# New orders of steps in four stages of a two-block transformer kernel

## The chip, the cores and the metric

The kernel runs as one launch on one core of a Trainium2 chip. The metric is device time in microseconds (us); lower is better.

## The reference

512 tokens of 1024 channels in float32 go through two blocks. The first is adaLN, one input projection, stick-breaking attention beside a Mamba-2 recurrence (SSD), and an output projection. The second is RWKV-7 time mixing, a convolutional FFN, sparse attention that chooses keys by an index score, and another FFN. Cut to what the four stages compute:

```python
# attention and SSD
log_beta = jax.nn.log_sigmoid(z)
log_one_minus = jnp.where(mask, jax.nn.log_sigmoid(-z), 0.0)
tail = lax.cumsum(log_one_minus, axis=3, reverse=True) - log_one_minus
weights = jnp.exp(jnp.where(mask, log_beta + tail, -jnp.inf))
y = ssd_scan(xs, dt, a, b_in, c_in, d_skip)
# time mixing: the front (shift, mix, projections), then the recurrence
xx = token_shift(x) - x
xm = x[None] + xx[None] * mix[:, None, None, :]
r, k, v = jnp.einsum('nbsd,nde->nbse', xm[:3], w_rkv)
state = (state * w_t[:, :, None, :] + sa[..., None] * b_t[:, :, None, :]
         + v_t[..., None] * k_t[:, :, None, :])
# sparse attention
score = jnp.einsum('bths,bth->bts', jax.nn.relu(s_idx), wi_b)
_, sel = lax.top_k(score, topk)
o_lat = jnp.einsum('bhtk,btkc->bthc', p, kv_sel)
```

## The kernel before

The program goes through its stages one after the other: input projection (to 112 us of the profiled execution), attention and SSD (112 to 475), output projection with its residual (475 to 587), the front of time mixing (587 to 697), the recurrence with time mixing's output projection (697 to 1140), the first FFN (1140 to 1570), sparse attention (1570 to 1819) and the last FFN (1819 to the end).

Each matrix product is made of three: a weight tile `raw` comes by a DMA that SP issues, ACT copies it to a rounded half `whi` (L213; in the front L1107), DVE or POOL subtracts to get the rest `wlo` (L216; L1109), and PE multiplies `whi` by the input's half `xh`, `whi` by `xl` and `wlo` by `xh` (L229, L229, L230). `raw` has three buffers, `whi` and `wlo` two each (four where the stage has room).

In four stages the work is split into generators, and a string of letters with counts says whose next step is written when: `run_order` (L119) takes a letter, and asks that generator for as many steps as the count says; what is left over at the string's end is written then. Within these stages the order of PE, DVE, ACT and POOL is the written one, so each engine works through its own list from the top and stops at an instruction that waits. The generators are:

- attention (`ATT_ORDER`): d dense products of the projection, z scores of a unit (L619 to L630), t its transposes (L641 to L647), v its product with the values (L660), g gates, s SSD.
- the front (`FRONT_ORDER`): t first half of a mixed input tile (DVE L1034 makes `xf`, ACT L1043 rounds it to `xh`), u its lower half `xl` (L1064, on POOL or DVE), v tiles of the values' input, w weights, d dense products, e their copies and the hidden layers (ACT L1167 to L1176, DVE L1161 to L1180), r the rest of the stage before: the norm's factors of the second 256 tokens (`factors2`, DVE L788 to L794, from sums that ACT makes in L779), their transposes (PE L802, then DVE L810 or ACT L807), and the four residual rows (ACT L815, then POOL L816).
- the recurrence (`ORDER`): l the small products of decay and rate (PE L1376 and L1377, ACT L1381, POOL L1383), p preparation of a unit of 64-token chunks (PE L1401 and L1411, DVE L1404 to L1455, ACT L1428, POOL L1451), g its pairwise products (PE L1474), i and h, v its triangular inverses, f and c the fold and the chain over chunks, t the tail, x input tiles for the second 256 tokens, d dense products of keys, values and the output. The first inverse of a unit is 14 pairs of small POOL instructions, L1515 and L1517, each dependent on the one before. `x` shares POOL with it: DVE makes `xf` (L1232, L1233; two buffers), ACT rounds it (L1220), POOL subtracts (L1221), and only then is the buffer free again. The result of a product of 256 columns and eight input tiles (48 matmuls L229 and L230) is copied out of its bank by ACT (L1259).
- sparse attention (`DSA_ORDER`): the steps of projection, index scores, choice, softmax, transposes and values, beside dense products.

A letter has no price of its own: a `d` in the recurrence is three matmuls, in attention also three but of twice the columns.

## Time and profile before

| | |
|---|---|
| median of 3 runs | 2213.78 us |
| lowest and highest run | 2212.26 and 2217.73 us |
| profiled execution, its own time | 2211.11 us |
| its span, first to last instruction | 2209.3 us |
| mean granted TensorE clock | 0.937 of full |
| PE busy | 1955.3 us, 89% of the span |
| DVE, ACT, POOL busy | 1462.7, 940.3, 902.8 us |

The busy shares are means over stages with different limits; the clock is the share of full speed that the throttle granted to PE.

### The profile page before, as it was taken

Reading aid. Unit: us, or ns where it says so; the run is one execution under the profiler, and the core shown is the slowest. Engines: PE = TensorE matmul, PEld = TensorE weight load, DVE = VectorE, ACT = ScalarE, POOL = GpSimd, SP = SyncE. Lnnn points to the kernel's source line nnn. Section 1 sums busy time; section 2 is a strip of 40 time slices with the busy share of each in tenths; the row PEclk is TensorE's granted clock in tenths of the full one; section 3 lists DMA queues with packets and bytes.
Section 4 is the critical chain, followed back from the end, with each engine's and each line's share of the span. In section 5 each row is a group of like instructions: output and inputs, shape, how many; then the busy total and the mean of one; then the engine's idle time right before and its main releaser. Section 6 shows DMA issues by size and latency. Waiting matters only on the chain.

```text
span 2209.3 us, 35729 instructions
## 1 busy us (share of the span) xinstructions
PE 1955.3 (89%) x14064; PEld 1631.0 (74%) x14064; DVE 1462.7 (66%) x2824; ACT 940.3 (43%) x1633; POOL 902.8 (41%) x787
## 2 busy tenths in 40 slices
...
GB/s 277 97 82 80 86 78 76 87 96 96 95 117 93 74 66 83 74 71 98 74 123 144 105 99 100 96 96 65 150 29 58 68 117 84 96 96 96 153 115 57
DMA packets 88856, 212.44 MB, mean 96 GB/s; under 512 B 23728, under 2 KB 36192, under 8 KB 88688
## 3 DMA queue, kind: packets, MB, share of 16 engines
...
q14 instruction: 57, 0.47, 0.1%
...
## 4 chain that ended last, share of the span: by engine, by line
PE 35%; DVE 14%; issue 8%; POOL 6%; ACT 3%; DMA 2%; POOLq 0%; DVEq 0%; ACTq 0%; SPq 0%
PE ps_pj L229 8%; PE ps_acc L229 7%; PE ps_pj L230 4%; PE ps_acc L230 3%; PE ps_w L229 3%; POOL wlo L216 2%; PE ps_w L230 1%; PE ps_kp L229 1%; DVE wlo L216 1%; POOL B L1517 1%; POOL b L1515 1%; ACT whi L213 1%; DVE rs_t L319 1%; DVE rs_t L320 1%; DMA raw<-in_w_up_dram 1%
## 5 line engine op out<-in xcount | busy, mean ns | idle before, releaser
L216 POOL TENSOR_TENSOR wlo<-raw,whi 128x1024 fp32r<-128x1024 f32 (+2 forms) x153 | 371.4, 2428 | 773.7 <-ACT whi L213 744.1
L213 ACT ACTIVATE whi<-raw 128x1024 fp32r<-128x1024 f32 (+2 forms) x276 | 290.0, 1052 | 491.9 <-PE ps_w L230 225.0
L216 DVE TENSOR_TENSOR wlo<-raw,whi 128x1024 fp32r<-128x1024 f32 (+1 forms) x123 | 162.1, 1318 | 268.7 <-ACT whi L213 266.9
L229 PE MATMUL ps_pj<-hh,whi 128*128 128x512 f32 x368 | 156.3, 425 | 1.7 <-ACT whi L213 1.7
L1920 DVE SCALAR_TENSOR_TENSOR fc<-ps_acc,pv,fc 128x511 f32<-128x511 f32 x88 | 65.9, 749 | 133.2 <-ACT fc L1918 131.6
L230 PE MATMUL ps_pj<-hh,wlo 128*128 128x512 f32 x368 | 145.1, 395 | 1.7 <-DVE wlo L216 1.7
L229 PE MATMUL ps_pj<-hl,whi 128*128 128x512 f32 x368 | 144.5, 393 | 0.0
L229 PE MATMUL ps_w<-wlo,ah 128*128 128x512 f32 x352 | 136.9, 389 | 0.6 <-POOL wlo L216 0.6
L229 PE MATMUL ps_w<-whi,ah 128*128 128x512 f32 x352 | 136.9, 389 | 0.0
L230 PE MATMUL ps_w<-whi,al 128*128 128x512 f32 x352 | 136.8, 389 | 0.0
L229 PE MATMUL ps_kp<-xh,whi 128*128 128x256 f32 x256 | 86.2, 337 | 12.7 <-ACT v L1259 9.0
L628 DVE TENSOR_TENSOR_SCAN cx<-om,zero 128x127 f32<-128x127 f32 (+3 forms) x64 | 74.1, 1158 | 34.2 <-ACT om L626 34.0
L229 PE MATMUL ps_pj<-x0h,whi 128*128 128x512 f32 (+1 forms) x192 | 73.9, 385 | 11.1 <-DVE x0h L305 6.1
L230 PEld LDWEIGHTS ps_pj<-hh,wlo 128*128 128x128 f32 x368 | 69.5, 189 | 18.2 <-DVE wlo L216 2.5
L229 PEld LDWEIGHTS ps_pj<-hh,whi 128*128 128x128 f32 x368 | 70.8, 192 | 14.2 <-ACT whi L213 2.6
L230 PE MATMUL ps_kp<-xh,wlo 128*128 128x256 f32 x256 | 76.3, 298 | 3.4 <-DVE wlo L216 3.3
L229 PEld LDWEIGHTS ps_pj<-hl,whi 128*128 128x128 f32 x368 | 70.1, 190 | 10.7 <-issue 0.2
L229 PEld LDWEIGHTS ps_w<-wlo,ah 128*128 128x128 f32 x352 | 66.1, 188 | 14.6 <-POOL wlo L216 1.0
L229 PE MATMUL ps_kp<-xl,whi 128*128 128x256 f32 x256 | 76.5, 299 | 0.3 <-POOL xl L1221 0.3
L229 PEld LDWEIGHTS ps_w<-whi,ah 128*128 128x128 f32 x352 | 66.1, 188 | 13.8
L230 PEld LDWEIGHTS ps_w<-whi,al 128*128 128x128 f32 x352 | 66.1, 188 | 13.6
L229 PE MATMUL ps_pj<-x1h,whi 128*128 128x512 f32 (+1 forms) x192 | 72.2, 377 | 2.4 <-DVE x1h L305 2.4
...
## 6 DMA issues: line engine op xcount, KB each, us to landing
...
```

Of the source, the lines that this page charges most:

```text
L213: self.nc.scalar.activation(hi[:, :n], raw[:, :n], AF.Copy)
L216: eng.tensor_sub(lo[:, :n], raw[:, :n], hi[:, :n])
L229: return (mm(out, wh, xh, start=first, stop=False), mm(out, wh, xl, start=False, stop=False), mm(out, wl, xh, start=False, stop=last))
L230: mm(out, wl, xh, start=False, stop=last))
L319: nc.vector.tensor_mul(t, y, y)
L320: nc.vector.scalar_tensor_tensor(t, t, -0.5, v, op0=OP.mult, op1=OP.mult)
L628: nc.vector.tensor_tensor_scan(cx[:, :n - 1][:, ::-1], om[:, 1:n][:, ::-1], K.zero.to_broadcast([128, n - 1]), 1.0, OP.mult, OP.add)
L1515: nc.gpsimd.tensor_mul(v, B[:, :s, s:s + 1].to_broadcast([64, s, n]), B[:, s:s + 1, s + 1:].to_broadcast([64, s, n]))
L1517: nc.gpsimd.tensor_add(B[:, :s, s + 1:], B[:, :s, s + 1:], v)
L1920: nc.vector.scalar_tensor_tensor(t[:, j:], pm[:, :T - j], cw(2 - j), t[:, j:], op0=OP.mult, op1=OP.add)
```

## The change

Four strings are replaced by others with the same steps: `ATT_ORDER`, `FRONT_ORDER`, `ORDER` and `DSA_ORDER`. No instruction is added, removed or moved to another engine, except that ACT loads its function tables two times less (in attention). The first line of each string in the diff:

```diff
 ATT_ORDER = (
-    "sgd2sds3ds2d2sds2dgd2sdzdz5dzsdts2dtdt2dsdtdztdz2dzds2tztzdv2s2zstzdtd3s3dtdzdzdz2dtsdt2zd2s2dt2ds2zdv2zsg"
+    "sd2s2d2sgs4d2s2d3sd2zds2z2dzdsdz2dzszdsdtdtdszsdtdtvzgsdz2dtdsztdtztd2gs2d2stzdtz2sd2svs2tztd2szdtdtztd2vd"
...
 FRONT_ORDER = (
-    "w2tutdwdtudwtdwtd3tduwudwutwd3wdt2dudwtudwtd2wd3wduwd2wdutd3er2wd2w2dur2detr2wutvrdtudwurdtuvrvdudwdtvtvw"
+    "rwt2w2tu2duwd2td3twtd2uw2dwd4twd2uwtud3wud2twuw2dudtdtdudutduwd2wet2udtr2wu2drtdtudwred2wr2drwrvd2wv3tvu2d"
...
 ORDER = (
-    "lp2d2p2dlpd4lpd7pd2ldxd3plpd4p2d7pd3pgd2pgplpdpd5gd4pl2dpd2pd2gd4gd2ildlgxi2gpdp2ixpdx2d2ihd2xilp2xiphpxih"
+    "l2p2d2ldpdxldld2pdp2dpd6p2lpd5pd7pdp2d2gd3pdpdgd4ldp2gd6pgd2plgd4xigdilidhp3dxlpdid2hdidp2xdlpxi2d2xp2dipi"
...
 DSA_ORDER = (
-    "a4qa4qdqe4d2edrqrqd3e5qde2qeqdeqede6d2e3je2j3e2de2jde2j2e2j2e2je3je2j2e3je5dj4rjd2ekejdjke3jedkejd2k2j2kek"
+    "a2qa5raqdqrq2e4qeqe2de3de2d3ede2qed2qe2de6dj2de2j2e6jejejeje2jedej3ejeje6je2jdjdejk2ekedk2jdjkjk2je3jdkj2k"
...
```

Three places show what the strings do to an engine's list.

**The start of the front, DVE.** `r` is now the string's first letter. Before, after the first half's transposes (L810):

```order
L769 SCALAR_TENSOR_TENSOR mx<-ps_w,rs_y,gateb 128x512 x2
L810 TENSOR_TENSOR xT<-ps_w,pv 128x4x128 x2
L1052 TENSOR_SCALAR xx<-xT 128x1
L1054 TENSOR_TENSOR xx<-xT 128x255
L1034 SCALAR_TENSOR_TENSOR xf<-xx,pv,xT 128x256
```

Now:

```order
L769 SCALAR_TENSOR_TENSOR mx<-ps_w,rs_y,gateb 128x512 x2
L810 TENSOR_TENSOR xT<-ps_w,pv 128x4x128 x2
L788 TENSOR_TENSOR ssqb<-ssqx 128x2
L273 TENSOR_SCALAR rmsv<-ssqb 128x2
L316 TENSOR_SCALAR rs_i<-rmsv 128x2
L317 TENSOR_SCALAR rs_y<-rs_i 128x2
...
L794 TENSOR_SCALAR dg<-cst,rs_y 128x128 x2
L1052 TENSOR_SCALAR xx<-xT 128x1
L1054 TENSOR_TENSOR xx<-xT 128x255
L1034 SCALAR_TENSOR_TENSOR xf<-xx,pv,xT 128x256
```

Fifteen small instructions (three rounds of L319, L320, L321 are left out above) moved from some forty rows later to the place ahead of the first input tile. L788 needs the last of ACT's sums L779; on ACT the last L779 and eight L807 now stand ahead of the first L1043.

**The end of the front, POOL.** Before:

```order
L1064 TENSOR_TENSOR xl<-xf,xh 128x256 x5
L816 TENSOR_TENSOR xt_4198<-xt_4198,gateb 128x1024
L1064 TENSOR_TENSOR xl<-xf,xh 128x256
L816 TENSOR_TENSOR xt_4200<-xt_4200,gateb 128x1024
L1064 TENSOR_TENSOR xl<-xf,xh 128x256 x2
L816 TENSOR_TENSOR xt_4202<-xt_4202,gateb 128x1024
L150 MEMSET pad_6181 128x1
```

Now:

```order
L816 TENSOR_TENSOR xt_4198<-xt_4198,gateb 128x1024
L816 TENSOR_TENSOR xt_4200<-xt_4200,gateb 128x1024
L1064 TENSOR_TENSOR xl<-xx,xh 128x256
L1064 TENSOR_TENSOR xl<-xf,xh 128x256 x2
L1109 TENSOR_TENSOR wlo<-raw,whi 128x1024
L1064 TENSOR_TENSOR xl<-xf,xh 128x256 x2
L816 TENSOR_TENSOR xt_4202<-xt_4202,gateb 128x1024
L1064 TENSOR_TENSOR xl<-xf,xh 128x256 x4
L150 MEMSET pad_6181 128x1
```

The residual rows moved ahead: the last four `xl` are no longer broken by one, and none stands at the end. On ACT the last L815 and the copy L1090 moved in the same way ahead of the last eight L1043.

**The recurrence, ACT around the fourth copy of a product.** Before:

```order
L1428 ACTIVATE P<-s 128x256
L1429 ACTIVATE s<-s 128x256
L1640 ACTIVATE VU<-ps_gm 64x512 x2
L1220 ACTIVATE xh<-xf 128x256
L1649 ACTIVATE BT<-ps_gm 128x512 x2
L1220 ACTIVATE xh<-xf 128x256 x3
L1658 ACTIVATE Z<-ps_gm 128x512
L1428 ACTIVATE P<-s 128x256
L1429 ACTIVATE s<-s 128x256
L1259 ACTIVATE v<-ps_kp 128x512
```

Now:

```order
L1428 ACTIVATE P<-s 128x256
L1429 ACTIVATE s<-s 128x256
L1220 ACTIVATE xh<-xf 128x256
L213 ACTIVATE l2h<-raw 128x512
L1220 ACTIVATE xh<-xf 128x256 x2
L1428 ACTIVATE P<-s 128x256
L1429 ACTIVATE s<-s 128x256
L1220 ACTIVATE xh<-xf 128x256
L1259 ACTIVATE v<-ps_kp 128x512
```

Three L1220 stand before this piece in the old order and one in the new, so the copy stands behind seven of them before and behind five now, and no longer behind L1649 and L1658. On POOL the third `xl` (L1221), which the fifth L1220 needs, stands two pairs of L1515 and L1517 ahead of the inverse's end in the new order; the fifth, which the seventh needs, stood behind that end in the old. At the start of the recurrence PE's list has also moved: the first four L1376 and L1377 now stand ahead of L1401 (before: behind L1411), and between L1401 and L1411 stand 21 dense matmuls and four small ones, where six dense ones stood. On DVE the first L1425 stands behind L1414 in both orders, and L1414 needs L1411.

At attention's end ACT's list had the last L590 behind an L608, an L645 and an L213; now the last L590 stands behind an L645 and an L213, the L608 of the product before it some five rows earlier and its own behind it. DVE's last three, L595, L596 and L647, stand as before.

## Rows read from the trace of the kernel before

**Rows 1.** Busy time by stretch; columns: busy us (instructions), granted clock, DMA share, GB/s.

```profile
core 0: us, PE busy (x) PEld busy (x) DVE busy (x) ACT busy (x) POOL busy (x), PEclk, DMA share, GB/s
112.00:475.00 363.00, 328.45 (x1955) 259.04 (x1953) 268.36 (x420) 207.36 (x358) 92.06 (x46) 0.98 0.28 87
...
587.00:697.00 110.00, 88.90 (x608) 82.44 (x608) 99.82 (x139) 57.93 (x121) 68.02 (x59) 0.89 0.31 104
697.00:1140.00 443.00, 379.73 (x5872) 336.62 (x5872) 346.04 (x766) 184.06 (x352) 250.25 (x393) 0.91 0.27 82
...
1570.00:1819.00 249.00, 199.56 (x1268) 153.89 (x1267) 174.38 (x571) 143.88 (x334) 129.06 (x115) 0.88 0.24 77
```

**Rows 2.** PE's waits from 587 to 697 us: total us, times, longest us.

```profile
PE ps_acc L229 <- DVE xl L1064: 6.5, 7, 1.5
PE ps_acc L229 <- POOL xl L1064: 3.9, 3, 2.8
```

**Rows 3.** Timeline, front's start, DVE: start us, us, what, [idle before <- releaser].

```profile
578.52 0.16 DVE L788 TENSOR_TENSOR ssqb<-ssqx 128x2 f32<-128x2 f32 x1 [0.85 <-ACT mx L779]
...
581.09 0.48 DVE L794 TENSOR_SCALAR dg<-cst,rs_y 128x128 f32<-128x128 f32 x2
...
582.81 1.41 DVE L810 TENSOR_TENSOR xT<-ps_w,pv 128x512 f32<-128x512 f32 x2
...
591.16 1.22 DVE L1109 TENSOR_TENSOR wlo<-raw,whi 128x1024 fp32r<-128x1024 f32 x1 [2.16 <-ACT whi L1107]
```

**Rows 4.** Timeline, front's start, POOL and PE: the second half's sum and the first product.

```profile
583.76 2.66 POOL L778 TENSOR_TENSOR xt<-xt,mx 128x512 f32<-128x512 f32 x2
```

```profile
587.20 0.39 PE L229 MATMUL ps_pj<-xh,whi 128*128 128x256 f32 x1 [1.94 <-ACT xh L1043]
```

**Rows 5.** Timeline, front's end: POOL, then PE, DVE and ACT.

```profile
691.23 2.38 POOL L816 TENSOR_TENSOR xt<-xt,gateb 128x1024 f32<-128x1024 f32 x1 [1.78 <-ACT xt L815]
```

```profile
688.63 0.58 PE L229 MATMUL ps_acc<-xl,whi 128*128 128x256 f32 x1 [2.80 <-POOL xl L1064]
```

```profile
690.10 0.69 DVE L1162 SCALAR_TENSOR_TENSOR hw<-lf,hw 64x512 fp32r<-64x512 f32 x1
...
691.28 2.88 DVE L1162 SCALAR_TENSOR_TENSOR ha<-lf,ha 64x512 fp32r<-64x512 f32 x1
```

```profile
694.27 0.60 ACT L1172 ACTIVATE lf<-ps_acc 128x512 f32<-128x512 f32 x1 [1.31 <-DVE ha L1162]
```

**Rows 6.** Timeline, recurrence's start: PE, then DVE.

```profile
697.73 1.87 PE L1401 MATMUL ps_gm<-cst,tmp 128*128 128x2 f32 x8 [2.19 <-ACT tmp L1396]
...
703.52 0.58 PE L230 MATMUL ps_kp<-xh,wlo 128*128 128x256 f32 x1 [3.28 <-DVE wlo L216]
```

```profile
705.02 0.34 DVE L1414 COPY rn<-ps_gm 64x8 f32<-64x8 f32 x2 [0.84 <-PE ps_gm L1411]
709.28 0.69 DVE L1425 TENSOR_TENSOR_SCAN s<-cst,s 128x256 f32<-128x256 f32 x1 [3.92 <-POOL s L1383]
```

**Rows 7.** Timeline, recurrence, the fourth copy: POOL, ACT, PE.

```profile
758.29 0.72 POOL L1221 TENSOR_TENSOR xl<-xf,xh 128x256 fp32r<-128x256 f32 x1
```

```profile
764.25 0.58 ACT L1259 ACTIVATE v<-ps_kp 128x512 f32<-128x512 f32 x1
```

```profile
752.70 1.97 PE L1655 MATMUL ps_gm<-VU,Gz 64*64 64x64 f32 x32 [0.34 <-ACT BT L1649]
...
764.88 0.58 PE L229 MATMUL ps_kp<-xh,whi 128*128 128x256 f32 x1 [8.62 <-ACT v L1259]
```

**Rows 8.** Timeline, attention's end: PE, then ACT.

```profile
472.33 2.52 PE L660 MATMUL ps_po<-at,v 128*64 128x128 f32 x16 [2.98 <-DVE at L647]
```

```profile
466.75 0.63 ACT L608 ACTIVATE sq<-xbc 128x512 f32<-128x512 f32 x1 [3.71 <-DVE xbc L596]
```

**Rows 9.** Busy time by short stretch at the recurrence's start: PE's granted clock.

```profile
697.70:708.00 10.30, 6.98 (x31) 0.50 0.47 154
```

More of the change, by code (lines that the diff above doesn't have):

```diff
@@ L701 @@
 ATT_ORDER = (
-    "sgd2sds3ds2d2sds2dgd2sdzdz5dzsdts2dtdt2dsdtdztdz2dzds2tztzdv2s2zstzdtd3s3dtdzdzdz2dtsdt2zd2s2dt2ds2zdv2zsg"
-    "zds2zdsdszsd2gtzvd3ztdsdtdzdtst2dstzdsdztsvsvt2d2tdstz2dsz2dszsz2dgtzd2ztd2stztdvgv2tdtdzdztdstzdzstdtz2dt"
-    "d2tdtzsdzdvgstvtsdz3dstzds2td2ztz2sdtdvztv2tdtzd2ts2tdtd2tztd2szgz2tsd2tds2dv2t2dzstzdzszdszszd2tdvtzszdtd"
-    "tzd2szdztdztdt2dszdzdgszvt2vz3sdgdtdvtzvdsdzsdtdz2dtdtdgds2tst2dtdzdzd2sz2szdt2dvs2vds2ztdtzd2gz3tdts2d2td"
-    "svzdtszdtvzdvtdt2dz2dtstdsd2tzd2ztd2sdzdtzv2tsdztzdtgd2vgt2d2tzds4dtds2z2dz2dgtdvzvts2zdtdtdszdzd3z2tdtdtz"
-    "tdtzsd3tzdsv2t2d2ztdz3d2zdz2dgdtvsdsdt2dtvtdtd2stz3dsdsgsdtd4td3vsd3sd66vdtd11sd7tds2tsd6vd2s2dsdvd4tsd3sd"
-    "sd2zsd5vd10sd3s"
+    "sd2s2d2sgs4d2s2d3sd2zds2z2dzdsdz2dzszdsdtdtdszsdtdtvzgsdz2dtdsztdtztd2gs2d2stzdtz2sd2svs2tztd2szdtdtztd2vd"
+    "ts2vzdtdgsvdtzs2tsdtz2d3gzdgt2sdsdzszdstdtz2dtdvtzvdstsz2dzdzts2dt2ds2gvzd2sz2dtdzs2t2sdzd2ztzvsvsz2dtd3t3"
+    "dztzdtzdz2d2sdtsdv2zdt2zsdt3dsgdtdtz2dtsdszdv2z2dz2dzt2d3szdzd2t2dtstdvztdtz2vtvs2zt2dtds2vtszdszdtdz2dsz2"
+    "sdtstdt2d2zdvstdstzd3gvsztd2zt2dv2d2zdztzdt2s3z3dzd2ztst2sdzdtztdzdszdtdzd2v2szsvdzstgtdztvz2d2t2zdtgd2t2s"
+    "dzt2zszds2zg2dgdts2tzd2zsdvtvzsd2tsdzsdsz2tdtsdtdztdsz2dzd2vd3vtstd2tdzd6t2dtz3dv2dsztz2dsdszdtdt2sgzdtzd3"
+    "stdsz2gztdsv2szdgd2s2tszd2vd2gt2dzsztd2tszd2s2dvsd2tztd2t2zdtzdt2d3sd6td6vd8td16sd3tdvtd3sd8s2dsd2sd21vd2"
+    "s3d3zd3sd3td12vd13zd15tvd3vs"
 )
```

34 lines of the change are left out of this document (17 added, 17 removed).

## The prediction

> **What bounds the kernel now.** No instruction comes or goes, so the change can only move waits. I read the busy time by stage first, then PE's waits, then the timelines of the places where the lists differ. The reader should see in the first that PE is the busy engine of three of the four stages and stands still for 363 - 328.45 = 34.6, 110 - 88.90 = 21.1, 443 - 379.73 = 63.3 and 249 - 199.56 = 49.4 us in them, 168 us in all [rows 1]; that is all an order can win besides the clock. In the front DVE is the busier one: 99.82 of 110 us. There PE's waits are many and small, 6.5 us in seven on DVE's `xl` and 3.9 in three on POOL's [rows 2]. A new string takes such waits away at some places and makes others; I therefore price the five places where the lists differ beside a wait of over 2 us, and leave the rest, with an even chance of both signs, to the range. PE's longest waits at the starts of attention and of sparse attention stand behind pieces of the lists that the strings leave as they were. The table loads that go are ACT's, which is busy 207.36 of 363 us [rows 1]: nothing.
>
> All is summed against the profiled execution's 2211.11 us; the median of the runs, 2213.78, lies 2.67 higher, which I add at the end.
>
> **1. The front's start.** The chain of the norm's factors ran from 578.52 to 581.09 + 0.48 = 581.57, 3.05 us, for the first half [rows 3]. Its twin for the second half now stands ahead of the first input tile. It cannot begin before POOL has made the second half's sum, which ends at 583.76 + 2.66 = 586.42 [rows 4], and ACT has squared it: about 587.0. DVE was free for the tile at 582.81 + 1.41 = 584.22 [rows 3]. So DVE stands 2.8 us and then works 3.05 on the factors, and the first product, which came at 587.20 [rows 4], comes up to 5.8 us later: the upper end. The lower end is DVE's own account: the 3.05 us are only done earlier, and the idle time of 2.16 us at 591.16 (it waited for `whi`, which stood on ACT behind eight L807 that now come sooner) goes [rows 3]; 2.8 - 2.16 = +0.6. As DVE is busy 91% of this stage, I stay nearer to its account: **+2.0**, ends +0.6 and +5.8.
>
> **2. The front's end.** PE waited 2.80 us at 688.63 for an `xl` that POOL had behind an L816; and the last L816, from 691.23 for 2.38 us, held DVE's L1162, which took 2.88 beside it and 0.69 a moment before, 2.2 us more; ACT's L1172 came at 694.27, when that was done [rows 5]. From there a single chain leads into the recurrence. In the new list no L816 stands in either place. The chain moves forward by 2.2, PE by 2.8 if the chain lets it: **-2.4**, ends -2.8 and 0.
>
> What hides a moved L816 is then the question. The row says that an L1162 beside it took 2.2 us more [rows 5]. The Trainium skill, "SBUF — State Buffer" (section "SBUF: two separate sides"), states that VectorE and GpSimd share one pair of ports as an exclusive lock, and that the one that comes second blocks for the whole instruction; the 2.88 us agree. By that rule DVE, nearly full here, would pay the 2.2 us wherever the L816 goes, and this term would be -0.2.
>
> **3. The recurrence's start.** The small products now precede L1401. That costs nothing, since PE waits there anyway: 2.19 us for L1401 and 3.28 for a `wlo` at 703.52 [rows 6]. It brings POOL's L1383 forward, for which DVE's L1425 stood 3.92 us until 709.28. But L1425 stands behind L1414, which came at 705.02 after L1411 [rows 6], and L1411 now stands behind 21 + 4 matmuls, of which 23 come after 703.52. In this stretch 31 rows of matmuls took 6.98 us at a granted clock of 0.50 [rows 9], 0.225 each: 23 take 5.2, so L1411 comes at 708.7 and L1425 hardly earlier than before. At full clock they take 2.6, and it comes some 2.3 us earlier. One wait takes the other's place: **-1.0**, ends -2.3 and 0.
>
> **4. The fourth copy in the recurrence.** PE waited 8.62 us until 764.88 for ACT's copy L1259 at 764.25, which had to come after the seventh input tile and so after POOL's fifth `xl`, at 758.29 + 0.72 = 759.0 [rows 7]. In the new list it needs the third `xl`, ahead of the inverse's end, so it loses up to 764.25 - 759.0 = 5.2 us. Against it: the work that PE did meanwhile is less, as the L1655 of 1.97 us [rows 7] now stands behind the wait. If the copy stays late, that adds 2.0. I take half of the gain, since the product before the wait also ends earlier: **-2.6**, ends -5.2 and +2.0.
>
> **5. Attention's end.** PE waited 2.98 us at 472.33 for an L647; ACT's list was held 3.71 us at an L608 (466.75) with the last L590 behind it [rows 8], and L647 stands behind that L590's two followers on DVE. Now that L608 is earlier. What stays are the two DVE rows after L590: **-1.5**, half of the wait; ends -3.0 and 0.
>
> **Sum.** +2.0 - 2.4 - 1.0 - 2.6 - 1.5 = -5.5 us of waiting; the ends add to -12.7 and +7.8. A wait also costs clock: from 697.7 to 708 the engine had waited 2.19 + 3.28 = 5.47 us and ran at 0.50, so that 6.98 x 0.50 = 3.5 us of its work were lost [rows 6, 9], 0.64 us for each of waiting. With that -5.5 is -9.0, and 2211.11 - 9.0 + 2.67 gives 2205. The ends become -20.8 and +12.8, thus 2193 and 2227.
>
> **Rivals.** *The held instructions only change place* (no change). Term 2 is then -0.2 in place of -2.4, the sum -3.3, with the clock -5.4: 2208. For it speaks that DVE has only 10 us free in the front [rows 1], against it that many of its rows there have no POOL work beside them. It is what the rule of "SBUF — State Buffer" in the Trainium skill, told under 2, would make of the time.
>
> *POOL's L816 in the front's middle* (slower). One L816 ahead of an `xl` cost PE 2.80 us [rows 5]. The second and third now stand back to back within the front, and the fourth ahead of four `xl`. If two of them hold PE as that one did, 5.6 us come in, and the start costs its upper end, since DVE then has no time to give back: 5.8 + 5.6 - 1.0 - 2.6 - 1.5 = +6.3, with the clock +10.3: 2224. It decides once PE's waits on POOL's `xl` in the front pass 3.9 + 5.6 = 9.5 us. For it: DVE and POOL are the fullest engines here. Against it: a residual row waits for nobody, and its own consumers are far.
>
> *The strings win everywhere* (much faster): the four stages' 168 us fall by a tenth, 16.8 us, which with the clock is -27.6: 2186. Nothing in the rows asks for it but the size of the change.
>
> That the new strings do not do what they say I can exclude: the lists hold the same instructions in other places.
>
> **How the numbers follow.** A run of this kernel can tell about 0.3%, 6.6 us, from no change: below 2207 is faster, above 2220 slower. The forecast, 2205, and the much faster rival together have 0.45; no change (2208, and whatever the unpriced waits undo) 0.25; slower 0.30. The forecast lies near the border of faster, so the chance is split rather than piled on it. The range goes from 2188, close to the much faster case, to 2230, a little past the upper ends.
>
> **What would show it.** Right: the first product of the front 1 to 6 us later than its L810; no wait of over 2 us on an `xl` near the front's end and L1162 under 1 us; L1425 no more than 2.3 us earlier against the start of the recurrence; the wait on the fourth copy at 3 to 6 us in place of 8.62; the wait on the last L647 under 2 us. Wrong: idle time of PE in the four stages above 175 or below 150 us, or a difference that lies in sparse attention, for which I priced nothing.

## The result, and the profile after

The changed kernel took 2234.59 us in the median of six runs (2223.78 to 2240.68), the kernel before 2214.35 in six beside them (2208.93 to 2217.73): a ratio of 1.0088, interval [1.0059, 1.0117]. It is slower, by some 20 us, where 2205 was forecast, and lies outside the range of 2188 to 2230. The same kernel was timed once more with the experiments (all_new below): 1.0058 [1.0041, 1.0076]. Both say slower; the second has eleven runs behind it and the narrower interval.

The profiled execution of the changed kernel has a span of 2237.0 us, and these engines' busy times on its page:

```profile
PE 1977.0 (88%) x14064; PEld 1643.9 (73%) x14064; DVE 1441.7 (64%) x2824; ACT 939.1 (42%) x1631; POOL 903.2 (40%) x787
```

To compare stages one needs marks that mean the same in both kernels. I take four stretches from an instruction of PE to another: attention (first L870 to first L694), the front (first L802 to first L1401, or after the change to the L1376 that now stands ahead of it), the recurrence (from there to the first L288 on `res`), sparse attention (first L2088 to the first L288 on `dres`). PE's busy time by stretch, first of the kernel before, with the granted clock behind the count:

```profile
core 0: us, PE busy (x), PEclk, DMA share, GB/s
121.10:479.50 358.40, 331.13 (x1958) 0.98 0.28 86
581.40:697.70 116.30, 92.77 (x641) 0.90 0.31 107
697.70:1140.30 442.60, 379.95 (x5872) 0.91 0.28 82
1570.70:1819.10 248.40, 198.86 (x1265) 0.88 0.24 77
```

and of the changed one:

```profile
123.70:483.60 359.90, 333.87 (x1959) 0.97 0.27 86
584.30:699.30 115.00, 90.06 (x642) 0.90 0.33 108
699.30:1153.60 454.30, 390.41 (x5873) 0.88 0.27 80
1586.50:1838.40 251.90, 208.84 (x1266) 0.84 0.23 72
```

PE's idle time in the four stretches was 27.3 + 23.5 + 62.7 + 49.5 = 163.0 us and is 26.0 + 24.9 + 63.9 + 43.1 = 157.9. That it fell is the doing of the last mark, the first L288 on `dres`. A long wait of PE lay just ahead of that mark in the kernel before and lies behind it now; first before, then changed:

```profile
1819.12 5.24 PE L288 MATMUL ps_t<-cst,dres 128*128 128x128 f32 x24 [6.73 <-DVE dres L2219]
```

```profile
1838.37 1.91 PE L288 MATMUL ps_t<-cst,dres 128*128 128x128 f32 x16
1847.85 1.94 PE L288 MATMUL ps_t<-cst,dres 128*128 128x128 f32 x8 [7.58 <-DVE rs_y L317]
```

Counted to the last L288 on `dres`, the four stretches have 166.0 us of idle time before and 168.6 after, and the whole span has 254.0 and 260.0. What grew more is the busy time for the same matmuls: by 10.5 us in the recurrence and by 10.0 in sparse attention (7.7 to its last L288), at a granted clock of 0.88 in place of 0.91 and 0.84 in place of 0.88; over the whole span by 21.7. Most of the time went into the clock, and little into waits.

The places that the prediction had priced look like this after the change. PE's timeline at attention's end, the front's start, the front's end, and the recurrence [rows 8, 4, 6, 7]:

```profile
476.69 1.95 PE L660 MATMUL ps_po<-at,v 128*64 128x128 f32 x16 [2.90 <-DVE at L647]
...
594.47 0.58 PE L229 MATMUL ps_pj<-xh,whi 128*128 128x256 f32 x1 [6.30 <-ACT xh L1043]
...
699.29 0.38 PE L1376 MATMUL ps_pj<-hw,l2h 128*128 128x256 f32 x1 [2.60 <-ACT l2h L213]
701.08 0.58 PE L1377 MATMUL ps_pj<-hw,l2l 128*128 128x256 f32 x1 [1.41 <-POOL l2l L216]
701.89 1.70 PE L1401 MATMUL ps_gm<-cst,tmp 128*128 128x2 f32 x8
...
763.75 1.97 PE L1489 MATMUL ps_gm<-cst,ar 64*64 64x64 f32 x32 [10.63 <-ACT BT L1649]
```

DVE's timeline at the front's start, its end and the recurrence's start [rows 3, 5, 6]:

```profile
589.93 0.16 DVE L788 TENSOR_TENSOR ssqb<-ssqx 128x2 f32<-128x2 f32 x1 [2.82 <-ACT mx L779]
...
695.42 0.69 DVE L1162 SCALAR_TENSOR_TENSOR ha<-lf,ha 64x512 fp32r<-64x512 f32 x1
...
710.64 0.34 DVE L1414 COPY rn<-ps_gm 64x8 f32<-64x8 f32 x2 [3.70 <-PE ps_gm L1411]
711.01 0.69 DVE L1425 TENSOR_TENSOR_SCAN s<-cst,s 128x256 f32<-128x256 f32 x1
```

One caution came out of the traces. The profile of a kernel in which only sparse attention was new was 15 us behind the kernel before when that stage *began*, with the same instructions up to there. One pair of traces therefore does not tell which stage a difference of 10 us comes from, and the study starts by timing the parts.

### The profile page after: what moved, and what is told of

The parts are those of the page before. It is cut to its first block, busy times and chain, and to the rows that moved or that the text cites. A ratio compares the mean times of both kernels' runs of the same rounds, so it can differ in the third digit from the quotient of the medians.

```text
span 2237.0 us, 35751 instructions
## 1 busy us (share of the span) xinstructions
PE 1977.0 (88%) x14064; PEld 1643.9 (73%) x14064; DVE 1441.7 (64%) x2824; ACT 939.1 (42%) x1631; POOL 903.2 (40%) x787
## 4 chain that ended last, share of the span: by engine, by line
PE 39%; DVE 11%; issue 9%; POOL 5%; ACT 3%; DMA 1%; SPq 0%; POOLq 0%; DVEq 0%; ACTq 0%
PE ps_pj L229 8%; PE ps_acc L229 7%; PE ps_pj L230 4%; PE ps_acc L230 3%; PE ps_w L229 3%; POOL wlo L216 3%; PE ps_kp L229 2%; PE ps_w L230 1%; PE ps_kp L230 1%; PE ps_z L2123 1%; PE ps_gm L1474 1%; DVE wlo L216 1%; DVE rs_t L319 1%; DVE rs_t L320 1%; ACT L L2355 1%
## 5 line engine op out<-in xcount | busy, mean ns | idle before, releaser
L216 POOL TENSOR_TENSOR wlo<-raw,whi 128x1024 fp32r<-128x1024 f32 (+2 forms) x153 | 370.5, 2422 | 785.9 <-ACT whi L213 755.4
L213 ACT ACTIVATE whi<-raw 128x1024 fp32r<-128x1024 f32 (+2 forms) x276 | 290.2, 1053 | 491.9 <-PE ps_w L230 227.3
L216 DVE TENSOR_TENSOR wlo<-raw,whi 128x1024 fp32r<-128x1024 f32 (+1 forms) x123 | 162.9, 1324 | 284.5 <-ACT whi L213 281.5
L229 PE MATMUL ps_pj<-hh,whi 128*128 128x512 f32 x368 | 158.8, 432 | 1.7 <-ACT whi L213 1.7
L229 PE MATMUL ps_pj<-hl,whi 128*128 128x512 f32 x368 | 146.4, 398 | 0.0
L229 PE MATMUL ps_w<-wlo,ah 128*128 128x512 f32 x352 | 137.7, 392 | 2.4 <-POOL wlo L216 2.4
L229 PE MATMUL ps_w<-whi,ah 128*128 128x512 f32 x352 | 136.8, 390 | 0.0
L229 PE MATMUL ps_kp<-xh,whi 128*128 128x256 f32 x256 | 88.3, 345 | 5.5 <-ACT v L1259 2.7
L229 PE MATMUL ps_pj<-x0h,whi 128*128 128x512 f32 (+1 forms) x192 | 73.5, 383 | 12.2 <-DVE rs_y L321 6.9
L229 PEld LDWEIGHTS ps_pj<-hh,whi 128*128 128x128 f32 x368 | 71.4, 194 | 15.9 <-ACT whi L213 2.6
L229 PEld LDWEIGHTS ps_pj<-hl,whi 128*128 128x128 f32 x368 | 71.1, 193 | 10.8 <-issue 0.2
L229 PEld LDWEIGHTS ps_w<-wlo,ah 128*128 128x128 f32 x352 | 66.6, 189 | 16.6 <-POOL wlo L216 2.8
L229 PE MATMUL ps_kp<-xl,whi 128*128 128x256 f32 x256 | 78.4, 306 | 0.0
L230 PEld LDWEIGHTS ps_w<-whi,al 128*128 128x128 f32 x352 | 66.5, 189 | 13.7
L229 PEld LDWEIGHTS ps_w<-whi,ah 128*128 128x128 f32 x352 | 66.2, 188 | 13.9
L229 PE MATMUL ps_pj<-x1h,whi 128*128 128x512 f32 (+1 forms) x192 | 72.2, 376 | 3.0 <-DVE x1h L305 3.0
```

The lines of the kernel that those rows point to most:

```text
L213: self.nc.scalar.activation(hi[:, :n], raw[:, :n], AF.Copy)
L216: eng.tensor_sub(lo[:, :n], raw[:, :n], hi[:, :n])
L229: return (mm(out, wh, xh, start=first, stop=False), mm(out, wh, xl, start=False, stop=False), mm(out, wl, xh, start=False, stop=last))
L230: mm(out, wl, xh, start=False, stop=last))
```

## The experiments

Each run was timed in five rounds beside the kernel before; ratios are against it.

| kernel | what is new | ratio | interval |
|---|---|---|---|
| only_att | attention's string | 0.9974 | [0.9953, 0.9996] |
| only_front | the front's string | 1.0000 | [0.9977, 1.0023] |
| only_wkv | the recurrence's string | 1.0032 | [1.0011, 1.0053] |
| only_dsa | sparse attention's string | 1.0035 | [1.0012, 1.0057] |
| all_new | all four | 1.0058 | [1.0041, 1.0076] |
| wkv_head | recurrence, to the third unit | 0.9981 | [0.9961, 1.0000] |
| wkv_mid | recurrence, to the sixth unit | 1.0040 | [1.0017, 1.0064] |
| wkv_wlo | recurrence, three L216 on DVE | 0.9995 | [0.9976, 1.0014] |
| dsa_head | sparse attention, to its first softmax step | 1.0034 | [1.0016, 1.0053] |
| dsa_early | sparse attention, to the third weight | 1.0017 | [0.9996, 1.0038] |
| dsa_late | sparse attention, from the third weight on | 1.0013 | [0.9990, 1.0036] |
| dsa_late2 | sparse attention, from the choice on | 1.0017 | [0.9992, 1.0042] |
| att_front_r | attention; the front with its `r` put back | 0.9988 | [0.9966, 1.0010] |
| att_wkvhead | attention; recurrence to the third unit | 0.9964 | [0.9943, 0.9986] |

### Which of the four strings

Each kernel takes one string of the change and leaves the others as they were. The first line of each string stands for it.

```diff
 ATT_ORDER = (
-    "sgd2sds3ds2d2sds2dgd2sdzdz5dzsdts2dtdt2dsdtdztdz2dzds2tztzdv2s2zstzdtd3s3dtdzdzdz2dtsdt2zd2s2dt2ds2zdv2zsg"
+    "sd2s2d2sgs4d2s2d3sd2zds2z2dzdsdz2dzszdsdtdtdszsdtdtvzgsdz2dtdsztdtztd2gs2d2stzdtz2sd2svs2tztd2szdtdtztd2vd"
...
```

> Only attention's order is new. Theory A (the loss sits in the recurrence and sparse attention): within 3 us of the kernel before. Theory B (each of the four orders carries about a quarter of the 20 us): 5 us slower. The traces of before and after put attention at 358.4 and 359.9 us between the first L870 and the first L694, which is +1.5.

Measured: 0.9974 [0.9953, 0.9996], 2209.75 us in the median: some 4 to 6 us faster, which neither theory had.

```diff
 FRONT_ORDER = (
-    "w2tutdwdtudwtdwtd3tduwudwutwd3wdt2dudwtudwtd2wd3wduwd2wdutd3er2wd2w2dur2detr2wutvrdtudwurdtuvrvdudwdtvtvw"
+    "rwt2w2tu2duwd2td3twtd2uw2dwd4twd2uwtud3wud2twuw2dudtdtdudutduwd2wet2udtr2wu2drtdtudwred2wr2drwrvd2wv3tvu2d"
...
```

> Only the front's order is new. Theory A: within 3 us of the kernel before; PE's wait for the first product about 6 us in place of 1.94, and as much given back by the end of the front. Theory B: 5 us slower. My forecast priced the front's start at +2.0 and its end at -2.4.

Measured: 1.0000 [0.9977, 1.0023]. Its first product waits 6.29 us, as in the changed kernel, and the front is as long as before, 116.1 us against 116.3.

```diff
 ORDER = (
-    "lp2d2p2dlpd4lpd7pd2ldxd3plpd4p2d7pd3pgd2pgplpdpd5gd4pl2dpd2pd2gd4gd2ildlgxi2gpdp2ixpdx2d2ihd2xilp2xiphpxih"
+    "l2p2d2ldpdxldld2pdp2dpd6p2lpd5pd7pdp2d2gd3pdpdgd4ldp2gd6pgd2plgd4xigdilidhp3dxlpdid2hdidp2xdlpxi2d2xp2dipi"
...
```

> Only the recurrence's order is new. Theory A: 10 to 13 us slower, with a wait of about 10 us at L1489 for ACT's copy L1649 where the wait of 8.6 us for the copy L1259 was, and the granted clock from 60 to 200 us into the stage below 0.85. Theory B: 5 us slower. The forecast's terms 3 and 4 would make it 3.6 us of waiting faster.

Measured: 1.0032 [1.0011, 1.0053]. The wait at L1489 that theory A names is there, with 10.49 us; the loss, some 7 us by the ratio, is less than its 10 to 13.

```diff
 DSA_ORDER = (
-    "a4qa4qdqe4d2edrqrqd3e5qde2qeqdeqede6d2e3je2j3e2de2jde2j2e2j2e2je3je2j2e3je5dj4rjd2ekejdjke3jedkejd2k2j2kek"
+    "a2qa5raqdqrq2e4qeqe2de3de2d3ede2qed2qe2de6dj2de2j2e6jejejeje2jedej3ejeje6je2jdjdejk2ekedk2jdjkjk2je3jdkj2k"
...
```

> Only sparse attention's order is new. Theory A: 5 to 9 us slower (the traces put the stage and the residual sum behind it at +8.7). Theory B: 5 us slower. The forecast priced nothing here: 0.

Measured: 1.0035 [1.0012, 1.0057]. So attention gains, the front does nothing, and both others lose. The four add to -0.26 + 0.00 + 0.32 + 0.35 = +0.41%. Whether they also add on the chip is told by the changed kernel itself, timed with the next group:

```diff
 ATT_ORDER = (
+    "sd2s2d2sgs4d2s2d3sd2zds2z2dzdsdz2dzszdsdtdtdszsdtdtvzgsdz2dtdsztdtztd2gs2d2stzdtz2sd2svs2tztd2szdtdtztd2vd"
...
 FRONT_ORDER = (
+    "rwt2w2tu2duwd2td3twtd2uw2dwd4twd2uwtud3wud2twuw2dudtdtdudutduwd2wet2udtr2wu2drtdtudwred2wr2drwrvd2wv3tvu2d"
...
 ORDER = (
+    "l2p2d2ldpdxldld2pdp2dpd6p2lpd5pd7pdp2d2gd3pdpdgd4ldp2gd6pgd2plgd4xigdilidhp3dxlpdid2hdidp2xdlpxi2d2xp2dipi"
...
 DSA_ORDER = (
+    "a2qa5raqdqrq2e4qeqe2de3de2d3ede2qed2qe2de6dj2de2j2e6jejejeje2jedej3ejeje6je2jdjdejk2ekedk2jdjkjk2je3jdkj2k"
...
```

> All four new orders, beside the next three kernels on one chip. Theory A (the four stages' effects add, and two of them carry the loss): the single orders measured -0.26, 0.00, +0.32 and +0.35%, so +0.41%, 9 us slower. Theory C (the orders hurt each other at the seams): the +0.88% of the first measurement, 19 us slower.

Measured: 1.0058 [1.0041, 1.0076]; the sum of the parts, 1.0041, is its lower bound. The parts add within their errors, which make about 0.44% for the sum, and there is no need of an interplay between the stages, though none is excluded.

Attention's gain, some 5.8 us by the ratio, does not show in its stretch, which is 357.1 to 360.4 us long in the traces with the new string and 356.1 to 361.4 in those with the old. A part of it lies ahead of the stretch: from the first L229 to the first L870, the same 156 matmuls, the five traces with the new string took 43.4 to 44.1 us, the eleven with the old 45.5 to 46.1. PE's wait ahead of that L870 is shorter, 5.09 to 6.06 us against 6.49 to 8.70; in the kernel before and in only_att:

```profile
121.11 0.77 PE L870 MATMUL ps_t<-xbc,xbc 128*128 128x128 f32 x2 [8.50 <-DVE xbc L838]
```

```profile
122.28 0.69 PE L870 MATMUL ps_t<-xbc,xbc 128*128 128x128 f32 x2 [5.09 <-DVE xbc L838]
```

By the stretch that is about 2 us; where the rest comes from stays open.

### The front's early `r`

The change puts the first step `r` (the second half's norm factors) at the head of the front's string. Here it stands behind the twelfth `t` again, as in the old string; attention's string is new too. The diff is against the new front.

```diff
 FRONT_ORDER = (
-    "rwt2w2tu2duwd2td3twtd2uw2dwd4twd2uwtud3wud2twuw2dudtdtdudutduwd2wet2udtr2wu2drtdtudwred2wr2drwrvd2wv3tvu2d"
+    "wt2w2tu2duwd2td3twtd2uw2dwd4twd2uwtud3wud2twuw2dudtdtdudutrduwd2wet2udtr2wu2drtdtudwred2wr2drwrvd2wv3tvu2dv"
...
```

> New orders for attention and the front, the others old, and the factors' step r moved from the front's head to behind its 12th input tile, about where the old order had it. If the 4.4 us that PE waits longer for the first product are only borrowed, as DVE's own account in the prediction had it: 0.25% faster than before, like attention's order alone. If they are a loss that another part of the new front's order makes up: 0.45% faster.

Measured: 0.9988 [0.9966, 1.0010]. With attention's share of 0.9974 taken off, putting `r` back wins nothing; in its one trace the front is 118.6 us long, against 116.1 with the early `r`. So the early `r` lent its time and is no loss, as term 1's account of DVE had it.

### The recurrence: where

The new order's first 167 steps, to the L1401 of the third unit, and then the old order without the steps already taken. The seam lies in this line, against the new string:

```diff
 ORDER = (
...
-    "x3phpdpxdxpd2xpxlhphpgxdvd2xhv2phgxphpx2dph2d2p2vld2vd3gldgpdvlgpd2vpgdldgdivdvgdfhdp2fpdgdgi2dpdf2ifdphdp"
+    "x3phpdpxdxpd2xpxlhphpgxdvd2xhv2phgxphpdhd2hpvxdlxlp2vlgdvg2d4gd2gdldvd2vdilpdpdgvid2fhp3fdifdpfidih2fphicd3"
...
```

> The recurrence's new order for its first 167 steps, to the third unit's L1401; behind it the old order without the steps already taken. Theory A1 (the new order wins 4 to 5 us in its first 70 us, as my terms 3 and 4 had it, and loses later): 4 us faster than before, with the third L1401 at 68 us after the first in place of 73. Theory A2 (the head only borrows, and the 10.6 us wait at L1489 comes with it): 3 to 7 us slower, as with the whole new order.

Measured: 0.9981 [0.9961, 1.0000]. The new beginning gains some 4 us, with a wait of 10.63 us at L1489 in its trace as well, so that wait by itself is not the loss. The loss lies behind it. The starts of L1401 show it unit by unit, in us after the first unit's:

| kernel | 2nd | 3rd | 4th | 5th | 6th | 7th | 8th unit |
|---|---|---|---|---|---|---|---|
| before | 42.7 | 73.3 | 106.8 | 152.8 | 199.3 | 245.3 | 290.6 |
| changed | 38.9 | 68.4 | 107.6 | 158.5 | 213.3 | 263.0 | 300.5 |
| all_new | 39.1 | 68.6 | 105.0 | 153.2 | 205.7 | 256.1 | 294.0 |
| only_wkv | 38.9 | 68.3 | 104.5 | 155.3 | 210.2 | 259.9 | 297.9 |
| wkv_mid | 38.9 | 68.4 | 104.8 | 153.0 | 205.4 | 253.3 | 292.7 |
| wkv_head | 38.9 | 68.4 | 104.1 | 147.5 | 195.0 | 242.8 | 282.2 |
| wkv_wlo | 38.8 | 68.2 | 104.6 | 152.6 | 199.4 | 249.1 | 285.4 |

The new order is 5 us ahead at the third unit and far behind at the seventh. From the fourth to the seventh unit the old order took 134.8 to 142.7 us in the eleven traces that have it there, the new 151.1 to 155.4 in three. To place the loss by time as well, the new order up to the sixth unit's L1401 (566 steps), then the old; the seam, against the new string:

```diff
 ORDER = (
...
-    "d3gvdhdviv2cp3cpidthsidhdfdhfd2pf2hpt2dchd4pd2ptdtfi2pcdfdiditdpihc2dipcd2gtdghpcphlp2dphtc2dld2ld2cxd2pxg"
+    "dhdviv2cp3cpidthsidhdfdhfd2pf2hpt2dchd4pd2ptdtfi2pcdfdiditdpihc2dipcd2gtdghpcphlp2dphtc2dld2ld2cxd2pxpcvcgv"
...
```

> The recurrence in its new order up to the sixth unit's L1401, then in the old order without the steps already done; all else old. The traces of the new order are ahead of the old at the third unit and 10 us behind at the fifth and sixth. Theory: the loss is made between the third and the sixth unit. Then the ratio is 1.003 to 1.005, and the sixth L1401 comes 255 to 260 us after the first (245 before). Rival: the traces only caught a dip of the clock there, and the loss lies in the last units: then it is 0.997 to 0.999, as for the new beginning alone.

Measured: 1.0040 [1.0017, 1.0064], and the L1401 of the seventh unit (the sixth after the first, which the expectation means) came at 253.3 us, a little ahead of the 255 to 260 expected. Within the errors the whole loss is made by the sixth unit; whether the new order's end changes anything is not shown.

### The recurrence: what

In the stretch from the fourth to the seventh unit, PE of the kernel before, of the changed one, and of the experiment below:

```profile
804.50:943.00 138.50, 125.79 (x2171) 0.95 0.26 77
```

```profile
809.50:964.90 155.40, 138.50 (x2165) 0.85 0.23 68
```

```profile
807.40:951.90 144.50, 129.52 (x2165) 0.92 0.26 73
```

Idle time grew by 16.9 - 12.7 = 4.2 us, busy time by 12.7. The largest new wait of PE there is for X, the first product of DVE's L1536 and L1542 at the head of the inverse's second half. DVE, then POOL, then PE, in the changed kernel:

```profile
860.24 1.37 DVE L1233 SCALAR_TENSOR_TENSOR xf<-x,pv,xf 128x256 f32<-128x256 f32 x1
861.53 3.17 DVE L1536 TENSOR_TENSOR T<-C,cst 128x128 f32<-128x128 f32 x2
864.73 0.45 DVE L1542 STREAM_TRANSPOSE X<-T 128x256 f32<-128x256 f32 x1
```

```profile
861.29 2.53 POOL L216 TENSOR_TENSOR wlo<-raw,whi 128x1024 fp32r<-128x1024 f32 x1
```

```profile
865.23 1.05 PE L1547 MATMUL ps_db<-X,NT 32*32 32x16 f32 x64 [3.01 <-DVE X L1542]
```

The same pair in the kernel before, and POOL around it:

```profile
849.83 0.48 DVE L1536 TENSOR_TENSOR T<-C,cst 128x128 f32<-128x128 f32 x2
```

```profile
850.64 1.28 POOL L216 TENSOR_TENSOR l2l<-raw,l2h 128x512 fp32r<-128x512 f32 x1 [1.01 <-ACT l2h L213]
...
852.62 2.53 POOL L216 TENSOR_TENSOR wlo<-raw,whi 128x1024 fp32r<-128x1024 f32 x1
```

The pair was through 0.3 us before the first L216 began; now it begins 0.24 us after the long one and ends 0.88 us after that one's end at 863.82. This happens three times: to the second unit's pair (2.75 us), the third's (3.17) and the fifth's (3.35), where the old order shows 0.91, 0.48 and 0.49. The Trainium skill, "SBUF — State Buffer" (section "SBUF: two separate sides"), states that a VectorE operation with two inputs in SBUF and a GpSimd operation that reads there take one pair of ports in turn, the later one blocked for the whole of the other's instruction. L1536 has two such inputs, and its rows agree: the pair ended behind the long L216 and not beside it. And then PE's clock, in stretches of 5 us around that wait in the changed kernel:

```profile
854.90:859.90 5.00, 4.06 (x67) 1.00 0.01 3
859.90:864.90 5.00, 2.33 (x28) 0.87 0.21 56
864.90:869.90 5.00, 4.67 (x138) 0.50 0.31 105
869.90:874.90 5.00, 5.00 (x45) 0.50 0.02 3
```

Two stretches of nearly full work follow at 0.50. So the candidate is one contention with a price in clock behind it. The experiment keeps the new order in full and takes the three L216 off POOL:

```diff
         def load(n):
             self.nw += 1
-            self.ahead.append(self.K.weight(n, eng=self.nc.vector if self.nw % 2 else self.nc.gpsimd))
+            eng = self.nc.vector if self.nw % 2 or self.nw in (14, 18, 28) else self.nc.gpsimd
+            self.ahead.append(self.K.weight(n, eng=eng))
```

> The recurrence in the new order throughout, all else old, but the three L216 (128x1024) that run on POOL beside the L1536 of the second, third and fifth unit are put on DVE, where they cost 1.3 us each in DVE's own order and cannot run beside L1536. Theory: the contention of these two engines makes the loss between the third and the sixth unit, by delaying L1542 and so PE's L1547 by some 2.5 us three times, each followed by a stretch at half clock. Then the three pairs take 0.5 to 1.1 us in place of 2.75, 3.17 and 2.46, the sixth L1401 comes by 203 us after the first in place of 205 to 213, and the ratio falls from 1.0032 to 0.998 to 1.000. Rival: the loss is spread over many small waits, and the 4 us more on DVE make up for what is won: 1.002 to 1.004.

Measured: 0.9995 [0.9976, 1.0014], against 1.0032 with these three on POOL; the difference of 0.37% is 8 us, with about 0.28% of uncertainty. The three pairs took 0.86, 0.48 and 1.17 us, the sixth unit's L1401 came at 199.4. The 16 instructions of L1536 with their shortest, median and longest time in ns, in the kernel before, the changed one and this one (where the line is L1537):

```profile
L1536 DVE TENSOR_TENSOR T<-C,cst x16: 278/286/2190, 768.7 to 1073.5; 128x128 f32<-128x128 f32 x16
```

```profile
L1536 DVE TENSOR_TENSOR T<-C,cst x16: 259/549/2457, 766.2 to 1089.2; 128x128 f32<-128x128 f32 x16
```

```profile
L1537 DVE TENSOR_TENSOR T<-C,cst x16: 257/284/967, 766.9 to 1075.9; 128x128 f32<-128x128 f32 x16
```

The numbers came out as the contention theory had them (1.17 lies just above its 1.1, and its 2.46 is the longest single L1536; the pair took 3.35), and the 4 us more on DVE cost nothing visible. One rival comes with the edit: POOL is relieved of some 7 us of work. The traces speak against it. From the fourth to the seventh unit PE did not wait for POOL in only_wkv nor here, and DVE's waits for POOL are no shorter (4.6 us there, 6.2 here), while PE's waits for DVE fell from 9.7 to 5.9 us. That this contention makes most of the loss between the third and the seventh unit is shown; a rest stays, since the stretch is 144.5 us long now, where the old order took up to 142.7.

"Three times" is too much, though. Only the third unit's pair made PE wait for its L1547 (3.01 us); ahead of the second's and the fifth's PE had other work, and the fifth's comes behind the seventh L1401. Against only_wkv the experiment won 2.8 us from the fourth to the fifth L1401, 8.1 to the sixth and nothing to the seventh. So most of it goes with one wait and the half clock behind it; the three moves were not tried one by one.

### Sparse attention: where

The new order up to its first softmax step (188 steps), then the old; the seam, against the new string:

```diff
 DSA_ORDER = (
...
-    "e3kjekdjed2kejde2dek2dej2edekdkejk2ede2d2j2kedlkldrklkd4lrs2ls2ds2ls2dls3jds2tlts3rts3tltsr2s2dks2vltkdstl"
+    "e3kjekdjed2kejde2dek2dej2edekdkejk2ede2d2j2kedlkldrklkd4lrl4s2ls2dls3ds2ds3tsks2dlst3s2tsds2tvs2lts2lvlstrv"
...
```

> Sparse attention's new order for its first 188 steps (projection, index scores, choice of the second to fourth blocks), behind them the old order from the first softmax step. Theory D1 (half of the 7.7 us is lost in the scores and the choice, where PE ran at a granted clock of 0.50 for 20 us): 4 us slower, with the first L2326 at 78 us after the stage's first L2088 in place of 73. Theory D2 (the loss sits in the softmax part alone): the same as before within 2 us.

Measured: 1.0034 [1.0016, 1.0053], as much as the whole new string, with the first L2326 (the first softmax product) 77.8 us into the stage. By these times the loss is made in the scores and the choice. The traces put only a part of it there: from that product to the stage's last L288 the three with the whole new string took 199.7 to 200.0 us, dsa_head 197.0, and the nine with the old order 194.2 to 196.0. Two splits of that head follow, around the dense step that loads the stage's third weight. First the new order up to it, then the old:

```diff
 DSA_ORDER = (
-    "a4qa4qdqe4d2edrqrqd3e5qde2qeqdeqede6d2e3je2j3e2de2jde2j2e2j2e2je3je2j2e3je5dj4rjd2ekejdjke3jedkejd2k2j2kek"
+    "a2qa5raqdqrq2e4qeqe2de3de2d3ede2qed2qde5d2e3je2j3e2de2jde2j2e2j2e2je3je2j2e3je5dj4rjd2ekejdjke3jedkejd2k2j2"
...
```

> Sparse attention in its new order only up to the ninth dense step (the one that loads the third weight), then in the old order; all else old. Theory one: the loss is made here, because the third weight comes later (its whi stands on ACT behind more copies), PE stands 1.62 us for it after a thin stretch, and the granted clock then stays at 0.50 for 25 us, which carries the scores and the choice with it. Then 1.003, 0.50 from 35 to 60 us into the stage, and the first softmax product 77 to 78 us into it. Theory two: the loss is made in the choice, because copies of keys are set among its steps on DVE. Then 1.000, and 73 to 74 us.

Measured: 1.0017 [0.9996, 1.0038]; the clock was 0.50 from 35 to 55 us into the stage, and the first softmax product came at 79.3 us. And the old order up to it, then the new:

```diff
 DSA_ORDER = (
-    "a4qa4qdqe4d2edrqrqd3e5qde2qeqdeqede6d2e3je2j3e2de2jde2j2e2j2e2je3je2j2e3je5dj4rjd2ekejdjke3jedkejd2k2j2kek"
+    "a4qa4qdqe4d2edrqrqd3e5qde2qeqde3qe2de6dj2de2j2e6jejejeje2jedej3ejeje6je2jdjdejk2ekedk2jdjkjk2je3jdkj2ke3kje"
...
```

> The counterpart: sparse attention in its old order up to the ninth dense step, then in the new order to the end; all else old. Theory one (the pocket ahead of the third weight and the clock after it): 0.999 to 1.000, the clock at 0.8 from 35 to 60 us into the stage, the first softmax product 73 to 74 us into it. Theory two (the choice): 1.003 and 77 to 78 us. If both halves cost about half, the two causes add, and neither theory is the whole.

Measured: 1.0013 [0.9990, 1.0036], the clock at 0.50 from 35 to 60 us, the first softmax product at 77.4 us. By the ratios each half costs about half, the third case of the expectation, though both intervals hold 1. Neither theory foretold the clock: both halves show the half clock. What they have in common is told by PE's waits just ahead of it. In the changed kernel:

```profile
1620.86 0.39 PE L230 MATMUL ps_pj<-ckh,wlo 128*128 128x256 f32 x1 [1.62 <-POOL wlo L216]
```

in dsa_late:

```profile
1605.93 0.70 PE L2123 MATMUL ps_z<-ki,qi 64*128 64x256 f32 x2 [0.69 <-ACT qi L2111]
1609.34 0.39 PE L230 MATMUL ps_pj<-ckh,wlo 128*128 128x256 f32 x1 [0.87 <-POOL wlo L216]
1611.22 1.12 PE L2123 MATMUL ps_z<-ki,qi 64*128 64x256 f32 x2 [0.52 <-ACT rl L2126]
```

and in the kernel before:

```profile
1600.14 0.70 PE L2123 MATMUL ps_z<-ki,qi 64*128 64x256 f32 x2 [0.69 <-ACT qi L2111]
1603.55 0.39 PE L230 MATMUL ps_pj<-ckh,wlo 128*128 128x256 f32 x1 [0.88 <-POOL wlo L216]
```

The first two waits of dsa_late are those of the kernel before, to 0.01 us. It has one more, of 0.52 us. The stretches from 30 to 35 and from 35 to 45 us into the stage, before:

```profile
1600.70:1605.70 5.00, 4.12 (x23) 1.00 0.20 57
1605.70:1615.70 10.00, 8.94 (x28) 0.84 0.06 24
```

changed:

```profile
1616.50:1621.50 5.00, 3.38 (x17) 0.98 0.00 0
1621.50:1631.50 10.00, 9.43 (x27) 0.50 0.16 52
```

dsa_late:

```profile
1606.40:1611.40 5.00, 3.61 (x19) 1.00 0.18 50
1611.40:1621.40 10.00, 9.43 (x24) 0.50 0.07 27
```

The clock repeats over all sixteen traces: in the five with the wait of 1.62 us and in dsa_late it was 0.50 from 35 to 40 us into the stage, in the ten others it stayed at 1.00. The kernel before falls later, to 0.68 from 40 to 45 us. That suggested one more split, behind the place of this pocket, PE's short pause in otherwise full work.

### Sparse attention: the pocket

The old order to the first step of the choice (55 steps), then the new:

```diff
 DSA_ORDER = (
-    "a4qa4qdqe4d2edrqrqd3e5qde2qeqdeqede6d2e3je2j3e2de2jde2j2e2j2e2je3je2j2e3je5dj4rjd2ekejdjke3jedkejd2k2j2kek"
+    "a4qa4qdqe4d2edrqrqd3e5qde2qeqdeqede6d2e3j2e2j2e6jejejeje2jedej3ejeje6je2jdjdejk2ekedk2jdjkjk2je3jdkj2ke3kje"
...
```

> Sparse attention in its old order up to the first step of the choice (55 steps, 16 more than in the earlier split), then in the new order to the end; all else old. The earlier split differed from the old order by one more wait of PE, 0.52 us for an rl, 35 us into the stage, and the granted clock was 0.50 from there on for 20 us. Theory: that pocket and the clock after it make the loss. Then 35 to 40 us into the stage the clock is 1.00 as in the kernel before, the first softmax product comes 73 to 75 us into it, and the ratio is 0.998 to 1.000. Rival: the new order of the choice loses by itself: 1.001 to 1.003 and 77 us.

In its trace the extra wait is gone and the clock stays up:

```profile
1601.80:1606.80 5.00, 4.12 (x21) 1.00 0.12 21
1606.80:1616.80 10.00, 8.97 (x35) 1.00 0.10 42
```

The first softmax product comes 72.2 us into the stage (before: 73.3, changed: 77.9). So far the theory of the pocket holds. The ratio, 1.0017 [0.9992, 1.0042], cannot tell the two theories apart; the number itself is the rival's. The traces can say more here, since this stage repeats well: from its first L2088 to the end of the kernel, nine traces with the old order took 636.0 to 638.6 us, the three with the whole new order 646.9 to 650.5, dsa_head 645.8, dsa_early 643.6, dsa_late 643.7 and dsa_late2 642.4. Compared with the whole new string about half of the loss is gone, but so it is in dsa_late, which has the pocket. These two differ in some 16 steps, and the 5.2 us between their first softmax products have shrunk to 1.3 at the end, since from that product to the stage's last L288 dsa_late2 took 199.8 us, dsa_late 197.0 and the kernel before 196.0. And dsa_early, with the latest first softmax product of all, at 79.3 us, ends with them. So the extra wait and the half clock behind it are shown, but not that they make the loss: dsa_early makes up behind that product for much of what it lost ahead of it, and dsa_late2 loses some 4 us there. What makes the loss of sparse attention stays open.

### The parts that win, together

```diff
 ATT_ORDER = (
+    "sd2s2d2sgs4d2s2d3sd2zds2z2dzdsdz2dzszdsdtdtdszsdtdtvzgsdz2dtdsztdtztd2gs2d2stzdtz2sd2svs2tztd2szdtdtztd2vd"
...
 ORDER = (
+    "l2p2d2ldpdxldld2pdp2dpd6p2lpd5pd7pdp2d2gd3pdpdgd4ldp2gd6pgd2plgd4xigdilidhp3dxlpdid2hdidp2xdlpxi2d2xp2dipi"
+    "x3phpdpxdxpd2xpxlhphpgxdvd2xhv2phgxphpdhd2hpvxdlxlp2vlgdvg2d4gd2gdldvd2vdilpdpdgvid2fhp3fdifdpfidih2fphicd3"
...
```

> The new string of attention together with the new beginning of the recurrence (up to the third unit's L1401), all else in the old order. If each of the two gains is real and stays where it was found, they multiply: 0.9974 x 0.9981 = 0.9955 of the time before, some 10 us. The rival: each was partly the spread of the clock, and then the pair gives 0.998 or no difference at all.

Measured: 0.9964 [0.9943, 0.9986], 2206.51 us in the median against 2215.19. The two gains multiply to 0.9955, which the interval holds. This version is faster than both kernels.

## Why the prediction was wrong, point by point

**1, the front's start.** Right in mechanism: DVE stood 2.82 us for ACT's last sum (2.8 was worked out), and the first product came 4.4 us later against the front's start (10.2 us after it, 5.8 before), within the mark of 1 to 6. In the sum it was mis-sized: +2.0 was taken, and the length of the front shows 0. DVE's own account, the lower end of +0.6, was the nearer one.

**2, the front's end.** The rows went as forecast: no L816 stands there, both L1162 take 0.69 us, the wait of 2.80 for `xl` [rows 5] is gone. The gain is not there: only_front has a ratio of 1.0000 and the old length. POOL's `xl` cost PE 3.1 us at another place of the front, and PE now waits 2.60 and 1.41 us for `l2h` and `l2l` at the end. That is the rival in which held instructions only change place, and in the front it was right.

**3, the recurrence's start.** Right: L1425 comes 9.1 us after the first L1401 in place of 11.55, and that L1401 itself 1.3 us later, so 1.2 us are won (1.0 forecast); DVE's L1414 waits 3.70 us for L1411, as described.

**4, the fourth copy.** The copy came earlier, 60.4 us after the first L1401 in place of 66.5. The wait did not shrink: 10.63 us in place of 8.62 [rows 7], now for `BT`. The step left out what else stands on ACT's list, a `P` (L1428) ahead of the copy, which waited 5.25 us for DVE's L1425 of the next unit. Terms 3 and 4 together still came out in size: -3.6 was forecast, the second unit's L1401 is 3.8 us earlier after the first (2.5 after the front's start), and the new beginning alone gains 0.19%, 4 us. As the wait of term 4 grew, that agreement is in part luck.

**5, attention's end.** Wrong: 2.90 us in place of 2.98, where 1.5 us were to go. Attention gains 0.26% all the same, at places that no term names. About 2 us of it lie in the wait for `xbc` at its start, and of just these waits the prediction said that they "stand behind pieces of the lists that the strings leave as they were"; the string's first line differs there.

**The step that failed** is the one ahead of the terms: I priced "the five places where the lists differ beside a wait of over 2 us", left the rest "with an even chance of both signs, to the range", and sparse attention at nothing. The loss came from there: 0.32% with the recurrence's string, whose priced beginning gains 0.19%, and 0.35% with sparse attention's. The first could have been read beforehand: the price of a DVE operation beside a long POOL one stood in [rows 5] (2.2 us more), and I weighed it for the front alone. In the recurrence the new string sets long L216 of POOL beside the L1536 of three units. Their pairs took 1.8 to 2.9 us more, and one of them cost PE a wait of 3.01 us and 10 us at half clock; with these L216 on DVE the ratio fell from 1.0032 to 0.9995. For sparse attention the cause is not known beyond the half clock after a wait of 1.62 us in place of 0.88.

**The clock's price.** I added 0.64 us for each us waited, from one row [rows 9], as if the clock's loss were in proportion to the waiting (2.19 of the 5.47 us of waiting lie ahead of that row's stretch). From the fourth to the seventh unit it was 12.7 us for 4.2, about 3 for 1, and in sparse attention a wait of 0.52 us more stood ahead of 20 us at half clock. The sum of the waits did not give the price. For the same reason my mark for "wrong" was blind: idle time between 150 and 175 us in the four stages. It is 157.9 by my marks and 168.6 with sparse attention counted to its last L288, inside both times, in a kernel that is slower.

**The rivals.** POOL's L816 in the front's middle had the right sign and, at 2224, the nearest time, but not the cause: PE's waits on POOL's `xl` came to 4.1 us, and it needed 9.5. The strings do not win everywhere. Of the range, the upper end of 2230 was the ends of the five terms; it had nothing in it for the places that were not priced.
